# Spreading a recurrence head's steps unevenly over the next projections

## The chip, the cores and the metric

The kernel runs on one core of one Trainium2 chip. The metric is the device time of one launch in microseconds (us). A kernel's figure is the median of several runs. The profile is of one further execution, with a time and a span of its own.

## The reference, cut to what matters

The reference is one inference step of a two-layer decoder trunk for a prompt of 1,024 tokens and 8 sample tokens: first a layer with a gated linear recurrence (HGRN2), then a layer with latent attention, each with a gated feed-forward part behind it. The change touches the first layer's recurrence alone. Its input is projected to four parts (query q, forget gate f, value i, output gate g) of 8 heads of 128. Then per head, in chunks:

```python
b = jnp.cumsum(gc, axis=2)                       # log of the forget gate, summed up
scores = jnp.einsum('bhtk,bhsk,bhtsk->bhts', qc, kc, decay)
o = (jnp.einsum('bhts,bhsv->bhtv', scores, vc)
     + jnp.einsum('bhtk,bhkv->bhtv', qc * jnp.exp(b), s))
s = (jnp.exp(b_last[:, :, 0, :, None]) * s
     + jnp.einsum('bhsk,bhsv->bhkv', kc * jnp.exp(b_last - b), vc))
```

Each head's output is normalised, gated with silu(g), and multiplied by an output matrix.

## The kernel before, in words

The kernel computes in float32. A projection's product is made of three matmuls per 128 rows of the model dimension (lines 181 to 183: both operands are split into a high and a low part). The 1,032 tokens are three spans of 344, so one projection of one span is 24 matmuls. A head has four weights in the order f, q, i, g, and so 12 such projections: f1, f2, f3, q1, q2, q3, i1, i2, i3, g1, g2, g3. In this document "a projection" is one of these 12, and a dash marks those of the next head (f1').

`proj(h)` is a generator with 12 units, one per projection. Each evicts its product on VectorE (L1035). Behind f3 stands a tail that forms b: a chain on ScalarE (L1052 to L1058) and VectorE (L1055 to L1060), and eight scans (L1065). Behind q3 stands a tail of two sigmoids on ScalarE (L1069, L1070) into the tile `sig`, and VectorE products that turn f into k, finish q and close the gate of the head before (L1072 to L1074, L1098). At g1 the values are turned on TensorE (L1087).

`rec(h)` is a generator with 26 steps that does the recurrence of one head, in chunks of 128 tokens, four chunks to a half:

- Seven levels per half (64, 32, 16, 8, 4, 2, 1). For each, `scaled` makes the tile X: a difference of b on VectorE (L1115), two exponentials on ScalarE (L1117), one product on GpSimd (L1118), one on VectorE (L1119). A matmul step of a level (L1129 for 64 and 32, L1145 for the small ones) reads it. `scaled` runs three levels ahead, so step 1 makes four of them, and each of the next steps one.
- `carry` moves the state through a half, in three parts. Part 1: difference (L1164), exponential (L1165), and on GpSimd the product kt (L1166). Part 2: four transposes of kt on TensorE (L1175) and a copy kn on ScalarE (L1177). Part 3: four matmuls with kn (L1182) and the state's update on VectorE (L1192). In half 0 the parts are issued in steps 4, 5 and 6, in half 1 in steps 12, 14 and 15.
- `outs` (L1204, L1206) in steps 12 and 20, and steps 8 and 17 with the level 0.
- `sample` for the 8 sample tokens: the old state is loaded (L1212) into the tile `sv`, scaled and updated (L1215 to L1217) and read by TensorE (L1223), all issued in step 18. Its transposes (L1229) come in step 19. `sv` and `sig` share one buffer (tag "big").
- `norm` in steps 21 to 26, two for each span: square, sum over partitions (L1243), reciprocal root on ScalarE, VectorE products (L1250 to L1252), split (L131 on ScalarE, L132 on GpSimd), stores.

The loop at the end of `hgrn` runs the projections of all heads in order and, behind each, as many recurrence steps as the table 'pace' says, first of the head before, then of the head itself. A head's first steps come behind its own i3, its last behind i3' of the next head: 13 projections. The last head keeps going behind the loop, mixed with products of the output projection.

The instructions are put in an order for each engine by a planner (the `TileContext` of the program is told to schedule with a timeline): instructions issued earlier go first, but one that is not ready in the planner's account can be overtaken. Each engine then runs its list in that order and waits where an operand is late. Buffers that share a tag are handed on when their last reader has finished.

Of the kernel before, what the change touches and what calls it, by code (L numbers as in the profile page):

```python
# [29 lines left out]
H = 8  # L30
# [238 lines left out]
def result(gen):  # L269
# [9 lines left out]
KN = {  # L279
# [3 lines left out]
    'fills': (2, 3, 4, 5, 7, 8, 10, 11, 12, 13),  # L283
    'early': (8, 1),
    'ev': (0, 0, 1),
    'm1': 2,
    'm2': 3,
# [2 lines left out]
    'ho': 1,  # L290
    'groups': ((0, 4), (4, 7), (7, 8)),
    'brate': 2,
    'pace': (8, 26, 13),
    'ahead': 3,
    'pvl': 2,
    'pre': 0,
# [672 lines left out]
def hgrn(k, c, w_in, gnorm, lbl, state, load, st_p, st_s, o_dram, v_dram, out):  # L969
# [13 lines left out]
    with ExitStack() as st:  # L983
# [305 lines left out]
            yield  # L1289
            yield from norm()  # L1290

        (START, STEPS, SPAN), UNITS = KN['pace'], 12
        recs = {}
        for u in range(UNITS * H):
            h, i = divmod(u, UNITS)
            if i == 0:
                units = proj(h)
            next(units)
            if i == UNITS - 1:
                next(units, None)  # L1300
            for j in (h - 1, h):
                n = (u + 1 - UNITS * j - START) * STEPS // SPAN
                if j >= 0 and n > 0:
                    if j not in recs:
                        recs[j] = [rec(j), 0]
                    while recs[j][1] < n:
                        next(recs[j][0], None)
                        recs[j][1] += 1
# [710 lines left out]
def tile_yoco_step(ctx, tc, a, c, o, phases=("hgrn", "ffn0", "mla", "ffn1")):  # L2019
# [21 lines left out]
    for n, ph in enumerate(phases):  # L2041
# [17 lines left out]
        if ph == "hgrn":  # L2059
            od = dram.tile([H, 2, P, T], F32, name="od_a")  # L2060
            vd = dram.tile([H, NB, P], F32, name="vd")
            out = OutProj(k, a["w_out_a"][0], od)
            hgrn(k, c, a["w_in_a"][0], gnorm, lbl, a["state_hgrn"], load, o["state_hgrn_prompt"], o["state_hgrn_sample"], od, vd, out)
            r = out.run(end)
        elif ph == "mla":
            od = dram.tile([H, 2, P, T], F32, name="od_b")
            out = OutProj(k, a["w_out_b"][0], od)

            def first():
                k.accs = ()  # L2070
                k.open_x()
                out.acc = [k.new_acc() for s in range(NS)]
                yield from out.first2(3)

            mla(k, c, a, o, gain(1, 0), cols[:, 64:72], cols[:, 72:74], cols[:, 74:77], r, k.close_x, od, lambda: [out.weight(f) for f in range(3)], first())
            r = out.run(end)
        else:
            r = ffn(k, gated[ph], a["w_ffn_out"][l], g_d, end)
# [69 lines left out]
```

## Time and profile before

| | |
|---|---|
| median of 3 runs | 2902.22 us (2901.31 to 2907.77) |
| the profiled execution, its own time | 2909.61 us |
| its span, first to last instruction | 2907.8 us |
| TensorE (PE) matmul busy | 2735.8 us, 94% |
| VectorE (DVE) / ScalarE (ACT) / GpSimd (POOL) busy | 65% / 44% / 34% |
| mean granted TensorE clock | 0.97 of full speed |

The busy shares are means over the whole span. The recurrence layer is the first fifth of it, and its shares differ from the rest, so it is read by stretches. A wait is given to the instruction that ended last before it. "Granted clock" is the share of TensorE's full clock.

### The profile page before, as it was taken

Reading aid. Unit: us, or ns where it says so; the run is one execution under the profiler, and the core shown is the slowest. Engines: PE = TensorE matmul, PEld = TensorE weight load, DVE = VectorE, ACT = ScalarE, POOL = GpSimd, SP = SyncE. Lnnn points to the kernel's source line nnn. Section 1 sums busy time; section 2 is a strip of 40 time slices with the busy share of each in tenths; the row PEclk is TensorE's granted clock in tenths of the full one; section 3 lists DMA queues with packets and bytes.
Section 4 is the critical chain, followed back from the end, with each engine's and each line's share of the span. In section 5 each row is a group of like instructions: output and inputs, shape, how many; then the busy total and the mean of one; then the engine's idle time right before and its main releaser. Section 6 shows DMA issues by size and latency. Waiting matters only on the chain.

```text
span 2907.8 us, 58217 instructions
## 1 busy us (share of the span) xinstructions
PE 2735.8 (94%) x23252; PEld 2552.8 (88%) x23252; DVE 1880.4 (65%) x3396; ACT 1279.0 (44%) x2888; POOL 983.9 (34%) x894
## 2 busy tenths in 40 slices
PE   7988888889999999999999999878999999998998
PEld 7988888887899999999968899746789999998997
DVE  7888888863585555555568888794358555555555
ACT  7666666654534444400155666523353444440102
POOL 3555555552343323322231111242135333232210
PEclk9999999989999999999999999999999999999999
DMA  5122222153323343544332112586432333436332
GB/s 185 53 68 68 65 68 65 60 185 99 107 91 108 99 114 93 152 160 156 127 99 81 40 45 74 189 335 211 131 106 77 106 105 100 116 118 232 133 124 74
DMA packets 302609, 335.77 MB, mean 115 GB/s; under 512 B 51266, under 2 KB 277104, under 8 KB 290688
## 3 DMA queue, kind: packets, MB, share of 16 engines
q1 hardware_dynamic: 277072, 263.15, 28.9%
q0 software_dynamic: 7456, 43.00, 4.0%
q10 hardware_dynamic: 17808, 25.89, 2.5%
q8 instruction: 183, 3.00, 0.4%
q14 instruction: 90, 0.74, 0.1%
HBM read 241.37 MB, written 90.61 MB: 114 GB/s over the span
## 4 chain that ended last, share of the span: by engine, by line
PE 67%; DVE 13%; ACT 7%; DMA 6%; issue 4%; POOL 2%; SPq 0%; DVEq 0%; POOLq 0%; ACTq 0%
PE ps L181 19%; PE ps L182 18%; PE ps L183 18%; DMA raw<-in_w_ffn_in_dram 3%; PE ps L1700 2%; PE ps L256 1%; DVE w L132 1%; DVE E L1115 1%; PE ps L1627 1%; POOL S L624 1%; DVE X L1119 1%; PE ps L1145 1%; DMA G<-g_d 1%; PE ps L1182 1%; DVE t L659 1%
## 5 line engine op out<-in xcount | busy, mean ns | idle before, releaser
L181 PE MATMUL ps<-xh,w 128*128 128x344 f32 (+1 forms) x2496 | 794.8, 319 | 6.2 <-DVE t L732 2.4
L182 PE MATMUL ps<-xl,w 128*128 128x344 f32 (+1 forms) x2496 | 777.0, 312 | 1.7 <-DVE xl L226 1.6
L183 PE MATMUL ps<-xh,w 128*128 128x344 f32 (+1 forms) x2496 | 772.3, 310 | 0.0
L157 POOL TENSOR_TENSOR w<-raw,w 128x512 fp32r<-128x512 f32 (+1 forms) x216 | 287.6, 1352 | 732.4 <-ACT w L153 715.6
L181 PEld LDWEIGHTS ps<-xh,w 128*128 128x128 f32 x2496 | 478.0, 192 | 29.1 <-issue 12.4
L182 PEld LDWEIGHTS ps<-xl,w 128*128 128x128 f32 x2496 | 477.9, 191 | 14.8 <-issue 6.9
L183 PEld LDWEIGHTS ps<-xh,w 128*128 128x128 f32 x2496 | 477.7, 192 | 6.3 <-issue 6.1
L822 DVE TENSOR_TENSOR acc<-ps,acc 128x344 f32<-128x344 f32 x432 | 222.6, 516 | 197.0 <-PE ps L183 197.0
L181 PE MATMUL ps<-G,w 128*128 128x344 f32 x1008 | 327.5, 325 | 13.6 <-DMA G<-g_d 13.5
L182 PE MATMUL ps<-G,w 128*128 128x344 f32 x1008 | 325.8, 323 | 0.0
L153 ACT CAST w<-raw 128x1024 fp32r<-128x1024 f32 (+4 forms) x134 | 130.2, 974 | 444.2 <-PE ps L183 269.8
L183 PE MATMUL ps<-G,w 128*128 128x344 f32 x1008 | 324.5, 322 | 0.0
L624 POOL TENSOR_TENSOR S<-raw 128x512 f32<-128x512 f32 x72 | 94.4, 1311 | 444.1 <-DMA raw<-in_w_ffn_in_dram 248.3
L132 DVE TENSOR_TENSOR w<-S,w 128x512 fp32r<-128x512 f32 x144 | 157.6, 1104 | 86.9 <-ACT w L131 86.8
L181 PE MATMUL ps<-X,w 128*128 128x258 f32 x720 | 206.4, 287 | 7.3 <-ACT t L721 5.9
L181 PEld LDWEIGHTS ps<-G,w 128*128 128x128 f32 x1008 | 191.6, 190 | 19.6 <-issue 17.8
L182 PE MATMUL ps<-X,w 128*128 128x258 f32 x720 | 204.2, 284 | 0.0
L183 PE MATMUL ps<-X,w 128*128 128x258 f32 x720 | 204.0, 283 | 0.0
L132 DVE TENSOR_TENSOR w<-raw,w 128x512 fp32r<-128x512 f32 x108 | 72.9, 689 | 188.4 <-ACT w L131 182.8
L182 PEld LDWEIGHTS ps<-G,w 128*128 128x128 f32 x1008 | 191.4, 190 | 2.0 <-issue 1.7
L183 PEld LDWEIGHTS ps<-G,w 128*128 128x128 f32 x1008 | 191.6, 190 | 1.1 <-issue 1.1
L181 PEld LDWEIGHTS ps<-X,w 128*128 128x128 f32 x720 | 137.7, 191 | 9.4 <-ACT t L721 6.1
(439 smaller groups left out, 6060.3 us busy)
## 6 DMA issues: line engine op xcount, KB each, us to landing
raw<-in_w_ffn_in_dram SPq DMA_DIRECT2D x88, 512.0 KB
G<-g_d SPq DMA_DIRECT2D x42, 1032.0 KB
g_d<-gs SPq DMA_DIRECT2D x108, 258.0 KB
raw<-in_w_ffn_out_dram SPq DMA_DIRECT2D x44, 512.0 KB
raw<-in_w_in_a_dram SPq DMA_DIRECT2D x32, 512.0 KB
xs<-x_d SPq DMA_DIRECT2D x72, 172.0 KB
x_d<-acc ACTq DMA_DIRECT2D x9, 1376.0 KB
g_d<-gs SPq DMA_DIRECT2D x108, 86.0 KB
```

Of the source, the lines that this page charges most:

```text
L132: (lo_eng or self.nc.vector).tensor_tensor(out=lo, in0=src, in1=hi, op=ALU.subtract)
L153: nc.scalar.copy(wh[:, :n], raw[:, :n])
L157: eng.tensor_tensor(out=wl[:, sl], in0=raw[:, sl], in1=wh[:, sl], op=ALU.subtract)
L181: nc.tensor.matmul(out, lhsT=wh, rhs=ah, start=first and i == 0, stop=False, **skip)
L182: nc.tensor.matmul(out, lhsT=wh, rhs=al, start=False, stop=False, **skip)
L183: nc.tensor.matmul(out, lhsT=wl, rhs=ah, start=False, stop=last and i == n - 1, **skip)
L256: k.nc.tensor.matmul(self.ps[32 * i:32 * i + 32, :W], lhsT=k.one[:, :32], rhs=self.ready[i], start=self.n == 0, stop=self.n == KC - 4, til ...
L624: nc.gpsimd.tensor_tensor(out=src[name], in0=src[a], in1=src[b], op=op)
L659: eng.tensor_tensor(out=part([out]), in0=part(a), in1=part(b), op=op)
L822: nc.vector.tensor_tensor(out=acc[s][:, dc, :], in0=po, in1=acc[s][:, dc, :], op=ALU.add)
L1115: nc.vector.tensor_tensor(out=pairs(E), in0=pairs(bv), in1=ref, op=ALU.subtract)
L1700: return lambda *a, **kw: self.tc.keep_in_program_order(getattr(self.eng, name)(*a, **kw))
```

## The change

The table 'pace' held a start, a number of steps and a span: from the 9th projection of a head on, two recurrence steps behind each projection. Now it holds for each of the 13 projections how many steps have been taken in all. The start and the end stay.

```diff
-    'pace': (8, 26, 13),
+    'pace': (1, 2, 3, 4, 6, 8, 11, 13, 16, 18, 21, 23, 26),
...
-        (START, STEPS, SPAN), UNITS = KN['pace'], 12
+        START, PACE, UNITS = 8, KN['pace'], 12
...
-                n = (u + 1 - UNITS * j - START) * STEPS // SPAN
+                n = u + 1 - UNITS * j - START
+                if n > 0:
+                    n = 2 * n if j == H - 1 or n > len(PACE) else PACE[n - 1]
```

Steps taken behind each projection of a head's run, before and after:

| | i3 | g1 | g2 | g3 | f1' | f2' | f3' | q1' | q2' | q3' | i1' | i2' | i3' |
|---|---|---|---|---|---|---|---|---|---|---|---|---|---|
| before | 1-2 | 3-4 | 5-6 | 7-8 | 9-10 | 11-12 | 13-14 | 15-16 | 17-18 | 19-20 | 21-22 | 23-24 | 25-26 |
| after | 1 | 2 | 3 | 4 | 5-6 | 7-8 | 9-11 | 12-13 | 14-16 | 17-18 | 19-21 | 22-23 | 24-26 |

The last head (j = H - 1) keeps two steps per projection. No instruction is added, removed or altered; only the order of issue changes.

## Rows read from the trace of the kernel before

**Rows 1.** Busy time by engine, with granted clock (PEclk), in two stretches of the span.

```profile
75.00:580.00 505.00, 458.34 (x5557) 429.41 (x5556) 414.59 (x642) 313.36 (x659) 268.61 (x217) 0.94 0.21 64
...
645.00:2908.00 2263.00, 2162.40 (x16581) 2016.67 (x16580) 1363.32 (x2571) 872.37 (x2044) 652.16 (x621) 0.98 0.38 123
```

**Rows 2.** TensorE's waits, 74 to 600 us: total, times, longest.

```profile
PE ps L1175 <- POOL kt L1166: 42.4, 8, 5.9
PE ps L1182 <- ACT kn L1177: 10.2, 8, 1.4
```

**Rows 3.** Busy time in six successive heads, from a third i projection's end to the next.

```profile
209.50:283.56 74.06, 66.73 (x810) 62.43 (x809) 60.60 (x94) 45.60 (x97) 39.70 (x33) 0.93 0.22 66
...
sum 444.30, PE 399.99 PEld 374.17 DVE 364.06 ACT 275.20 POOL 239.23; mean PE 66.67 PEld 62.36 DVE 60.68 ACT 45.87 POOL 39.87
```

**Rows 4.** Timeline of TensorE around one wait (start, duration, instruction, idle before).

```profile
221.04 0.44 PE L1145 MATMUL ps<-X 128*32 128x32 f32 x26
227.36 1.11 PE L1175 MATMUL ps<-ident,kt 128*128 128x128 f32 x4 [5.88 <-POOL kt L1166]
230.12 2.08 PE L1182 MATMUL ps<-vn,kn 128*128 128x128 f32 x8 [1.39 <-ACT kn L1177]
232.71 0.66 PE L181 MATMUL ps<-xh,w 128*128 128x344 f32 x1
237.89 0.46 PE L1145 MATMUL ps<-X 128*32 128x32 f32 x32
...
243.52 0.43 PE L181 MATMUL ps<-xh,w 128*128 128x344 f32 x1
247.50 0.46 PE L1145 MATMUL ps<-X 128*32 128x32 f32 x32
...
258.66 1.05 PE L1182 MATMUL ps<-vn,kn 128*128 128x128 f32 x8
```

**Rows 5.** Timeline of VectorE and GpSimd behind that wait.

```profile
222.42 0.68 DVE L1164 TENSOR_TENSOR E<-b 128x512 f32<-128x512 f32 x1
224.09 0.41 DVE L1119 TENSOR_TENSOR X<-lin,E 128x256 f32<-128x256 f32 x1
226.12 1.46 DVE L1119 TENSOR_TENSOR X<-lin,E 128x256 f32<-128x256 f32 x1 [0.82 <-ACT E L1117]
...
224.82 1.26 POOL L132 TENSOR_TENSOR ol<-oy,oh 128x344 fp32r<-128x344 f32 x1 [1.02 <-issue]
226.05 1.25 POOL L1166 TENSOR_TENSOR kt<-lin,E 128x512 f32<-128x512 f32 x1
```

**Rows 6.** Busy time and clock behind head 0's waits, and behind that of rows 4.

```profile
82.00:90.50 8.50, 8.39 (x69) 7.89 (x72) 8.50 (x13) 2.13 (x7) 5.07 (x5) 0.61 0.01 2
230.12:232.20 2.08, 2.08 (x13) 1.86 (x17) 2.08 (x3) 0.56 (x2) 2.07 (x3) 0.50 0.03 8
```

**Rows 7.** TensorE's waits in head 0, 60 to 137 us.

```profile
PE ps L1182 <- ACT kn L1177: 1.2, 1, 1.2
PE ps L1175 <- POOL kt L1166: 1.1, 1, 1.1
```

**Rows 8.** VectorE by line in one head, 209.5 to 283.56 us.

```profile
L1119 DVE TENSOR_TENSOR X<-lin,E 128x256 f32<-128x256 f32 x14 | 13.6, 990 | 1.0 <-ACT E L1117 0.8 <-PE ps L1129 0.2
L1115 DVE TENSOR_TENSOR E<-b 128x512 f32<-128x512 f32 x14 | 12.1, 880 | 0.2
...
L1035 DVE TENSOR_TENSOR lin<-ps,r 128x344 f32<-128x344 f32 x9 | 4.6, 507 | 5.3 <-PE ps L183 5.3
```

**Rows 9.** The state's load, the end of the gate, and the product that reads the state.

```profile
199.87 1.77 DVE L1098 SCALAR_TENSOR_TENSOR lin<-lin,gains,sig 128x1032 f32<-128x1032 f32 x1
201.78 0.37 SPq L1212 DMA_DIRECT2D sv<-in_state_hgrn_dram  x1
...
L1223 PE MATMUL ps<-sv,qpad x16: 272/273/295, 264.6 to 265.0; 128*32 128x128 f32 x16
L1215 POOL TENSOR_TENSOR sv<-sv,fs x1: 1962/1962/1962, 205.8 to 205.8; 128x1024 f32<-128x1024 f32 x1
```

## The prediction

> **What bounds the kernel now.** I read by stretches first. In the recurrence layer TensorE is busy 458 of 505 us at a granted clock of 0.94, behind it 96% at 0.98 [rows 1]. So the layer's heads, about 74 us each, are where TensorE stands still. TensorE's own waits come next: between 74 and 600 us nearly all of them have two names, the transposes of kt (42.4 us in 8) and the matmuls on kn (10.2 us in 8) [rows 2]. The timeline of one head gives their place. The transposes of half 0, issued in step 5 behind g2, wait 5.88 us. The kn matmuls behind them wait 1.39 us. Then the clock is down: the kn matmuls take 2.08 us where later ones take 1.05, and the projection behind (first matmul to what follows) 237.89 - 232.71 = 5.18 us where another takes 247.50 - 243.52 = 3.98 [rows 4]. The granted clock there is 0.50, the 1.2 GHz level, after TensorE stood idle for most of 9 us [rows 4, 6]. So one head loses 5.9 + 1.4 = 7.3 us in waits and 1.0 + 1.2 + about 0.2 for the small matmuls = 2.4 us in clock, together 9.7. That fits the head's length: 444.30 / 6 = 74.05 us, of which TensorE is busy 66.67 [rows 3], and 66.67 - 2.4 = 64.3 is its work at full clock.
>
> Why kt is late is seen on VectorE and GpSimd. VectorE comes to the carry's difference (L1164) only at 222.42, with TensorE idle since 221.48 [rows 4, 5]. GpSimd makes kt at 226.05, behind the split (L132, 224.82) of the norm of the head before [rows 5]. VectorE is busy 60.60 us of this head's 74.06, and 5.3 us of its rest lie before evictions, where it waits for TensorE [rows 3, 8]. The wait is thus a crowd: in two projections (i3, g1) the table before issues the first four steps, that is seven of the fourteen level tiles, beside the norm of the head before. One level costs VectorE (13.6 + 12.1) / 14 = 1.84 us [rows 8], so seven cost 12.9, and TensorE's projection lasts 3.98.
>
> **What the change does, part by part.** Nothing is added or removed; the sum is made of waits and clock.
>
> *Step 5, half 0.* It moves from behind g2 to behind f1', step 4 (which makes kt) from behind g1 to behind g3. TensorE has the same steps before it, and two projections more: it comes to the transposes not at 221.48 but 2 x 3.98 later, at 229.4. kt was ready at 226.05 + 1.25 = 227.3 [rows 4, 5]. VectorE has two more evictions before it (0.51 each [rows 8]): 228.3. So the 5.9 us go, with a margin of 1.1 us that the planner's order may eat. Bounds for what is left: 0 and 5.9; I take 0.3, near the computed end.
>
> *Step 6.* It stays behind the same projection as step 5, so the copy kn still stands between them with little to cover it. Bounds 0 and 1.4; I take 1.0, nearest to the row.
>
> *Half 1.* Steps 14 and 15 were behind different projections and are now behind one (q2'). So a wait like that of step 6 is added: 0 to 1.4, I take 0.6, since step 16's matmuls are issued there too and can be put between. The tiles of the second half are now made beside the tail behind f3', a long chain on ScalarE and VectorE, where before they lay ahead of it. Steps 9 to 11 add three levels, 5.5 us, there. The cover is that half 1's kt is still issued a whole projection ahead of its transposes; if it is gone, this is the wait of half 0 in a new place (the second rival's kind).
>
> *The clock.* In head 0 two short waits of 1.1 and 1.2 us [rows 7] are followed by a clock of 0.61 over 8.5 us [rows 6], so short waits can cost it too. Bounds 0 and 2.4, I take 1.2.
>
> *Queues.* No DMA is added; step 18's loads on SP are the ones that could move (second rival). GpSimd's products go with their levels, 39.70 us busy of 74.06 [rows 3], so room is left.
>
> What stays is 0.3 + 1.0 + 0.6 + 1.2 = 3.1 us a head, the gain 9.7 - 3.1 = 6.6. Six heads' waits (heads 1 to 6) are of the full kind: 39.6. Head 0 has 2.3 us of wait and, as in the others, about 2.4 of clock; I take half, 2.4. Head 7 keeps its old table, but shares i3 with three last steps of head 6 instead of two: it loses 0 to 1, I take 0.5. Sum 41.5 us. Nothing behind the layer hides it: TensorE is 96% busy there [rows 1], so what it saves is saved at the end. The profiled execution's 2909.61 becomes 2868; that execution lies 7.4 us over the median of the runs, 2902.22, which becomes 2861.
>
> **The rivals.**
>
> *VectorE becomes the bound.* Its 60.68 us of work a head [rows 3] don't shrink. Of its idle 13.4 us, 5.3 are waits for TensorE, which a faster TensorE takes away; the other 8.1 are waits on ScalarE and gaps. If those stay, a head can't fall below 60.7 + 8.1 = 68.8 us: a gain of 5.2 a head, 31 in six, 2871. If the new crowd behind f3' and q3' adds 3 us of waits to that, 72 us a head and some 2889. For it speaks that 60.7 us of work must fit beside TensorE's 64.3; against it, that the levels issued beside f3' can fill the waits of its chain on ScalarE. A page of the Trainium skill, GPSIMD Engine Reference, Specifications, says that GpSimd and VectorE share their way into SBUF, so that two-input VectorE instructions are slowed. By it the change, which takes away none of GpSimd's work, leaves VectorE's time as it is, and the end would be this rival's 2871. The trace agrees: the same product took 0.41 us with GpSimd idle and 1.46 us beside kt [rows 5].
>
> *Slower: the state's load goes behind the sigmoids.* `sv` and `sig` have one buffer. Before, step 18 was issued behind q2', ahead of the sigmoids of q3'; the load goes out at 201.78, as soon as the gate (L1098) has read `sig` at 201.64, 63 us ahead of the matmuls at 264.6 [rows 9]. Now step 18 is issued behind q3' and its tail. If the buffer is then handed out in order of issue, the load waits for the gate that follows q3'. That is 4.2 us or more behind q3': between its end and i3's end at 209.50 [rows 3] lie three projections, so it ended at 209.50 - 11.9 = 197.6 at the latest, and the load went out at 201.78. GpSimd's first product (L1215) began 4.0 us behind the load and took 1.96, and a second of the same size follows [rows 9]. So L1223 could start 4.2 + 4.0 + 1.96 + 1.96 = 12.1 us behind q3', and held in its place it costs that and 2.4 of clock, 14.5, for 9.7 saved: 4.8 a head lost, 34 in seven, 2936. It turns the sign from a wait of 7.3 us on. Against it: the load is taken far ahead of its issue, and the planner can put projections in front of a product that it knows to be late. Then it costs little.
>
> *No change.* The planner already takes work out of issue order (26 of the 32 records of step 5's small matmuls stand ahead of the transposes that it issues first [rows 4]). If it again leaves the first levels crowded, or the same wait comes back in half 1 (6 + 1.4 + 2.4), the time stays within some us of 2902.
>
> **How the numbers follow.** A measurement of this kernel tells 0.2%, about 6 us, from no change. Forecast, 2845 to 2875: 0.50. VectorE as the bound with waits left, 2875 to 2896: 0.27. No change, 2896 to 2908: 0.08. Slower by the load or a larger wait in half 1, 2908 to 2955: 0.15. So faster 0.77, same 0.08, slower 0.15. The range is 2845 to 2902: it leaves out the slower case and half of the unchanged one, 0.19.
>
> **What would show it.** In the changed profile: L1175 should wait under 1 us a head in place of 5.9, L1182 at most 1.4 in either half; the stretch behind should hold a clock of 1.00; a head from i3 to i3 should last 66 to 69 us with TensorE's work unchanged; VectorE's waits before evictions should shrink from 5.3 us. I am wrong if a new wait of over 3 us a head stands at L1175 behind q2', at L1223 or at L1204 behind i1', if the load L1212 is issued behind the gate of the next head, or if the slow clock stays although the waits are short.

## The result, and the profile after

The changed kernel takes 3052.95 us (median of 5 runs, 3049.72 to 3055.16) against 2902.22 (2901.31 to 2912.1): a ratio of 1.051, 95% interval 1.0496 to 1.0523. It is 151 us slower, where 41 us faster was forecast.

| | before | after |
|---|---|---|
| the profiled execution, its own time | 2909.61 us | 3053.28 us |
| its span | 2907.8 us | 3051.5 us |
| TensorE (PE) matmul busy | 2735.8 us, 94% | 2748.7 us, 90% |
| VectorE / ScalarE / GpSimd busy | 65% / 44% / 34% | 60% / 44% / 32% |
| mean granted TensorE clock | 0.97 | 0.951 |

The first view is busy time by stretches: one head of the changed kernel (start, end and length; then busy time of PE, PEld, DVE, ACT and POOL; then clock, DMA share, GB/s), the gap in it, and the projection behind the gap.

```profile
140.85:236.74 95.89, 69.23 (x811) 64.96 (x807) 56.00 (x93) 54.33 (x103) 38.44 (x32) 0.86 0.16 51
219.56:235.73 16.17, 0.00 (x1) 0.00 (x1) 5.74 (x8) 7.18 (x10) 7.95 (x5) 0.60 0.32 97
236.74:242.30 5.56, 5.56 (x31) 5.54 (x28) 0.04 (x1) 0.47 (x2) 0.00 (x0) 0.71 0.33 94
```

A head lasts 95.9 us at a clock of 0.86, where before it lasted 74.05 at 0.93 [rows 3]. For 16.2 us TensorE runs nothing, and the projection behind the gap takes 5.56 us. From one head's third i eviction to the next the trace has 95.6 us in the mean ((634.74 - 252.37) / 4); (95.6 - 74.05) x 7 heads = 151, about the whole loss. Work was added on ScalarE alone: 54.33 us busy in 103 instructions against 45.60 in 97 [rows 3].

TensorE's waits, 60 to 800 us (total, times, longest), answer to [rows 2, 7]:

```profile
PE ps L1223 <- POOL sv L1217: 113.9, 7, 16.6
PE ps L1182 <- ACT kn L1177: 72.5, 15, 7.1
PE ps L1175 <- POOL kt L1166: 3.5, 1, 3.5
```

The wait that the change was to remove is removed: 42.4 us for kt are now 3.5, and those are the last head's, which keeps its old table. But the kn matmuls wait 72.5 us instead of 10.2, and the state's matmuls, which did not wait, wait 113.9. The timeline of several engines shows how that big wait comes about (start, duration, engine, instruction, idle time before it and what ended that).

```profile
224.67 1.29 DVE L1098 SCALAR_TENSOR_TENSOR lin<-lin,gains,sig 128x1032 f32<-128x1032 f32 x1
...
226.09 0.37 SPq L1212 DMA_DIRECT2D sv<-in_state_hgrn_dram  x1
...
230.22 1.89 POOL L1215 TENSOR_TENSOR sv<-sv,fs 128x1024 f32<-128x1024 f32 x1 [2.89 <-DMA sv<-in_state_hgrn_dram]
...
231.46 1.73 DVE L1216 TENSOR_TENSOR sv<-sv,lin 128x1024 f32<-128x1024 f32 x1 [4.91 <-issue]
...
233.34 2.34 POOL L1217 TENSOR_TENSOR sv<-sv 128x1024 f32<-128x1024 f32 x1 [1.23 <-DVE sv L1216]
...
235.73 1.08 PE L1223 MATMUL ps<-sv,qpad 128*32 128x128 f32 x16 [16.17 <-POOL sv L1217]
```

The load of the state (L1212) leaves 0.13 us behind the end of the gate (224.67 + 1.29 = 225.96), as in [rows 9]. But the gate is now the one that follows q3', and the matmuls that need the load come next on TensorE, not 63 us later. From TensorE's last matmul ahead of the gap (219.56, of a step issued behind q3') to the load are 6.5 us, from there to GpSimd's first product 4.1, from there to the end of its second 5.5. No projection was put in front.

The timeline of ScalarE ahead of that, and behind it TensorE's row for half 1's kn:

```profile
193.77 0.63 ACT L1057 ACTIVATE tw<-tw 128x516 f32<-128x516 f32 x1
194.42 1.28 ACT L1069 ACT_TABLE_LOAD   x1
195.71 1.07 ACT L1069 ACTIVATE sig<-lin 128x1032 f32<-128x1032 f32 x1
...
197.47 1.28 ACT L1058 ACT_TABLE_LOAD   x1
198.77 0.63 ACT L1058 ACTIVATE tw<-tw 128x516 f32<-128x516 f32 x1
199.42 1.28 ACT L1165 ACT_TABLE_LOAD   x1
...
203.21 1.28 ACT L1054 ACT_TABLE_LOAD   x1
...
205.95 1.28 ACT L1167 ACT_TABLE_LOAD   x1
...
210.76 0.57 ACT L1177 COPY kn<-ps 128x512 f32<-128x512 f32 x1
211.35 1.28 ACT L1058 ACT_TABLE_LOAD   x1
...
211.38 2.08 PE L1182 MATMUL ps<-vn,kn 128*128 128x128 f32 x8 [7.07 <-ACT kn L1177]
```

The forecast had no term for this. The first sigmoid (L1069, into `sig`) now runs in the middle of f3''s chain of logarithms (L1054, L1058) and of exponentials (L1057, L1165 and L1167 among them). The kernel names one common activation table for those two in the line behind the sigmoids (L1071); ahead of it each change of kind costs a table load of 1.28 us. Four such loads lie between the sigmoid and the copy kn, and L1182 waits 7.07 us. The groups of table loads by line, of the kernel before and then of the changed one (times, busy time, mean ns of one), 75 to 700 us:

```profile
L1069 ACT ACT_TABLE_LOAD x7 | 9.0, 1283 | 0.1
L1071 ACT ACT_TABLE_LOAD x7 | 9.0, 1283 | 0.1
```

```profile
L1058 ACT ACT_TABLE_LOAD x14 | 18.0, 1283 | 0.2
L1069 ACT ACT_TABLE_LOAD x7 | 9.0, 1283 | 0.1
L1165 ACT ACT_TABLE_LOAD x7 | 9.0, 1283 | 0.1
L1054 ACT ACT_TABLE_LOAD x7 | 9.0, 1283 | 0.1
...
L1070 ACT ACT_TABLE_LOAD x7 | 9.0, 1283 | 0.1
```

Nine a head instead of two. Before, `sv` held the shared buffer until its matmuls (264.6, [rows 9]), so the sigmoids could not be early; in the runs below that issue step 18 or its load ahead of them again, the loads are back at two a head.

### The profile page after: what moved, and what is told of

Same layout as the page of the kernel before. It is cut to its first block, busy times and chain, and to the rows that moved or that the text cites. A ratio compares the mean times of both kernels' runs of the same rounds, so it can differ in the third digit from the quotient of the medians.

```text
span 3051.5 us, 58227 instructions
## 1 busy us (share of the span) xinstructions
PE 2748.7 (90%) x23252; PEld 2566.4 (84%) x23252; DVE 1845.6 (60%) x3396; ACT 1340.3 (44%) x2937; POOL 972.6 (32%) x894
## 4 chain that ended last, share of the span: by engine, by line
PE 60%; DVE 14%; ACT 12%; DMA 7%; issue 5%; POOL 3%; SPq 0%; DVEq 0%; POOLq 0%; ACTq 0%
PE ps L181 17%; PE ps L182 16%; PE ps L183 16%; DMA raw<-in_w_ffn_in_dram 3%; PE ps L1702 2%; DVE t L659 2%; PE ps L256 1%; DVE E L1115 1%; DVE X L1119 1%; DVE w L132 1%; PE ps L1629 1%; POOL S L624 1%; ACT E L1117 1%; DMA G<-g_d 1%; PE ps L1182 1%
## 5 line engine op out<-in xcount | busy, mean ns | idle before, releaser
L157 POOL TENSOR_TENSOR w<-raw,w 128x512 fp32r<-128x512 f32 (+1 forms) x216 | 295.2, 1387 | 714.5 <-ACT w L153 693.0
L181 PEld LDWEIGHTS ps<-xh,w 128*128 128x128 f32 x2496 | 484.3, 194 | 28.4 <-issue 13.2
L182 PEld LDWEIGHTS ps<-xl,w 128*128 128x128 f32 x2496 | 484.9, 194 | 14.2 <-issue 7.2
L183 PEld LDWEIGHTS ps<-xh,w 128*128 128x128 f32 x2496 | 483.2, 194 | 6.3 <-issue 6.1
L132 DVE TENSOR_TENSOR w<-S,w 128x512 fp32r<-128x512 f32 x144 | 157.6, 1104 | 82.2 <-ACT w L131 82.1
L132 DVE TENSOR_TENSOR w<-raw,w 128x512 fp32r<-128x512 f32 x108 | 73.0, 690 | 189.5 <-ACT w L131 184.1
L1118 POOL TENSOR_TENSOR X<-lin,E 128x256 f32<-128x256 f32 x112 | 105.0, 946 | 146.4 <-PE ps L1145 56.0
```

The costliest lines, as they stand in the source:

```text
L132: (lo_eng or self.nc.vector).tensor_tensor(out=lo, in0=src, in1=hi, op=ALU.subtract)
L157: eng.tensor_tensor(out=wl[:, sl], in0=raw[:, sl], in1=wh[:, sl], op=ALU.subtract)
L181: nc.tensor.matmul(out, lhsT=wh, rhs=ah, start=first and i == 0, stop=False, **skip)
L182: nc.tensor.matmul(out, lhsT=wh, rhs=al, start=False, stop=False, **skip)
L183: nc.tensor.matmul(out, lhsT=wl, rhs=ah, start=False, stop=last and i == n - 1, **skip)
L1118: nc.gpsimd.tensor_tensor(out=Xl[:, :, 0, :], in0=kl[:, :, 0, :], in1=El[:, :, 0, :], op=ALU.mult)
```

## The experiments

Some of the experiments ran beside a kernel before of 2902 to 2903 us, others (e4, e5, e7, e8, e13) beside one of 2915 to 2918. So runs of the two groups are compared by their ratios to the kernel before measured beside each.

### Step 18 back behind q2', and step 18 alone behind q3'

The first kernel takes step 18 out of the change, the second keeps nothing else of it.

```diff
-    'pace': (1, 2, 3, 4, 6, 8, 11, 13, 16, 18, 21, 23, 26),
+    'pace': (1, 2, 3, 4, 6, 8, 11, 13, 18, 18, 21, 23, 26),   # e1_step18_before
+    'pace': (2, 4, 6, 8, 10, 12, 14, 16, 17, 20, 22, 24, 26),  # e2_only18_late
```

> The changed table with one entry altered: behind q2' 18 steps are taken in all instead of 16, so that step 18 (the state's load into the buffer that sv and sig share) is issued ahead of q3' and its sigmoids again; all else as in the change. Theory A (the handing on of the shared buffer is the whole loss): L1223's wait of 16.2 us a head goes, the six to seven extra table loads a head on ScalarE go with it, L1182's 7.1 us behind q2' fall under 2, and the gain of the spread start appears: 2850 to 2885 us. Rival B (the crowd behind f3' and q1' to q2' is a loss of its own): L1223's wait goes, but L1182 still waits 5 to 7 us behind q2' and the clock stays down there: 2900 to 2960 us.

Measured: 2935.63 us, ratio 1.0114 (1.0092 to 1.0136). The waits of the first, 75 to 760 us:

```profile
PE ps L1182 <- ACT kn L1177: 81.1, 15, 8.1
PE ps L1175 <- POOL kt L1166: 4.0, 1, 4.0
```

L1223's wait is gone and the table loads are two a head again. That takes back 117 of the 151 us, but the rest of the table does not gain: it loses 33 us, in the range of rival B, since kn is waited for in both halves (8.0 us a head in half 0, 4.4 in half 1; rival B had put the larger wait in half 1). The timeline of ScalarE, VectorE and TensorE in half 0 of one head:

```profile
239.17 0.76 ACT L1117 ACTIVATE E<-E 128x256 f32<-128x256 f32 x2 [2.44 <-DVE E L1115]
241.94 0.42 ACT L1117 ACTIVATE E<-E 128x256 f32<-128x256 f32 x1 [2.00 <-DVE E L1115]
...
244.44 0.72 ACT L1117 ACTIVATE E<-E 128x256 f32<-128x256 f32 x2 [0.85 <-DVE E L1115]
246.12 0.72 ACT L1117 ACTIVATE E<-E 128x256 f32<-128x256 f32 x2 [0.95 <-DVE E L1115]
246.87 0.59 ACT L1177 COPY kn<-ps 128x512 f32<-128x512 f32 x1
...
237.72 4.19 DVE L1115 TENSOR_TENSOR E<-b 128x512 f32<-128x512 f32 x2
...
243.67 2.36 DVE L1115 TENSOR_TENSOR E<-b 128x512 f32<-128x512 f32 x2
...
238.50 0.60 PE L1175 MATMUL ps<-ident,kt 128*128 128x128 f32 x4
...
247.51 1.86 PE L1182 MATMUL ps<-vn,kn 128*128 128x128 f32 x7 [8.02 <-ACT kn L1177]
```

The transposes are done at 239.1. The copy that takes them over needs 0.59 us, but it stands on ScalarE behind the exponentials of four levels (L1117), each of which waits for a difference of VectorE (L1115), and a cast of a weight between them (1.03 us). It comes 7.8 us late. TensorE no longer waits for VectorE through kt; it waits for VectorE through ScalarE's queue.

> The table of before, two steps behind each projection, with one entry altered: behind q2' 17 steps in all instead of 18, so that only step 18 moves behind q3'. Theory A: this alone brings the loss: L1223 waits 14 to 17 us a head, the first sigmoid is taken early into the free buffer and ScalarE loads tables six to seven times more a head, the old wait of L1175 behind g2 stays in part: 3000 to 3060 us. Rival B: only L1223's wait comes, no wait of over 2 us at L1182 in half 1: 2990 to 3020 us. If the late step 18 were not the cause: 2895 to 2915 us.

Measured: 3054.86 us, ratio 1.0521 (1.0496 to 1.0547). The waits, 75 to 760 us:

```profile
PE ps L1223 <- POOL sv L1217: 156.0, 7, 22.4
PE ps L1175 <- POOL kt L1166: 20.7, 8, 4.0
PE ps L1182 <- ACT kn L1177: 13.1, 8, 2.5
```

One step moved by one projection brings a loss as large as that of the whole change, though with a longer wait (22.3 us a head) and with part of the old one for kt. The trace has eight table loads a head here.

### The first sigmoid kept in its place

The changed kernel, with the first sigmoid kept in program order on ScalarE.

```diff
-   nc.scalar.activation(out=sig[:, 0, :], in_=f, func=AF.Sigmoid, scale=-1.0)
+   tc.keep_in_program_order(nc.scalar.activation(out=sig[:, 0, :], in_=f, func=AF.Sigmoid, scale=-1.0))
```

> The changed kernel, with the first sigmoid (L1069) pinned behind everything issued before it on ScalarE, so that it can't be taken early; the order of the shared buffer stays that of the change. Theory A: table loads go back to two a head, L1182's wait behind q2' falls from 7.1 us to under 2, L1223's wait of about 16 us stays: 2985 to 3025 us. Rival B (the wait at L1182 comes from the crowd of levels and not from the loads): L1182 keeps 5 to 7 us: 3035 to 3060 us.

Measured: 3030.2 us, ratio 1.044 (1.0411 to 1.047). Two table loads a head; the waits, 75 to 760 us:

```profile
PE ps L1223 <- POOL sv L1217: 107.0, 7, 15.4
PE ps L1182 <- ACT kn L1177: 54.7, 15, 4.4
```

The early sigmoid with its seven extra loads a head costs 23 of the 151 us (3052.95 - 3030.2), above all through half 1's kn, whose wait falls from 7.1 to 4.4 us. That is less than was expected; the order in which the buffer is handed on is the larger part.

### The buffer taken earlier, the matmuls left where the change puts them

The changed table, but `sv` is taken from the pool and its loads are issued in step 15; products and matmuls stay in step 18.

```diff
+            def fetch():
                 big_ = gp.tile([P, 3, T], F32, name="sv", tag="big")
...
+                state_["sv"] = S0, vB
+
             def sample():
+                S0, vB = state_["sv"]
...
+                if (hf, hh) == (1, 2):
+                    fetch()
```

> The changed table as it is, step 18 behind q3' as in the change, but the shared buffer is taken for sv and the two loads into it are issued in step 15 (behind q2', ahead of the sigmoids of q3'); the products on it and L1223 stay in step 18. Theory A (the order in which the one buffer is handed on is the cause, not the place of step 18's matmuls): L1223 waits under 2 us a head, ScalarE loads tables twice a head, and the time is within 1% of the run with step 18 moved whole (ratio 1.0114): 1.004 to 1.020. Rival: the products behind q3' or L1223's place cost it, L1223 keeps 5 us or more a head and the ratio stays over 1.025.

Measured: 2975.21 us, ratio 1.0205 (1.0179 to 1.0232), a hair above the expected bound of 1.020. The loads go out far ahead again, behind the gate of the head before, as [rows 9] (the queue's own row), and of the waits, 75 to 760 us, L1223's is gone (lines behind 1213 are shifted by 4: L1233 is L1229, L1229 is L1225):

```profile
217.96 0.37 SPq L1212 DMA_DIRECT2D sv<-in_state_hgrn_dram  x1
```

```profile
PE ps L1182 <- ACT kn L1177: 75.6, 15, 7.4
PE ps L1233 <- ACT so L1229: 15.2, 7, 2.2
```

The table loads are two a head. So the issue order of the two users of one buffer is the cause of the wait, and not that step 18 lies behind q3' as such; that place costs the remaining per cent over the first experiment (2.2 us a head of it are the wait for `so`, the copy of what L1223 made).

### What makes kn late

First, step 6 a projection behind step 5, and the second half as before:

```diff
-    'pace': (1, 2, 3, 4, 6, 8, 11, 13, 18, 18, 21, 23, 26),   # the first experiment's
+    'pace': (1, 2, 3, 4, 5, 8, 11, 13, 18, 18, 21, 23, 26),   # e4_step6_apart
+    'pace': (1, 2, 3, 4, 6, 8, 11, 14, 18, 20, 22, 24, 26),   # e5_old_tail
```

> The table of the run with step 18 ahead of q3' (2935.6 us), and step 6 moved from behind f1' to behind f2' with steps 7 and 8, so that a whole projection lies between the transposes of kt and the matmuls on kn. Theory C (the wait only went from kt to its copy kn, because steps 5 and 6 share a projection and the copy stands behind exponentials on ScalarE): L1182's 8.0 us in half 0 fall to between 1 and 4.5, a head gets 3 to 6 us shorter, 2895 to 2918 us. Rival D (VectorE is late at this place whatever the order, and what is won at kn is lost at the next level's matmuls): other waits of the same sum appear at L1145 or L1129, 2925 to 2945 us.

> The spread start of the change (steps 1 to 11 as there), and from q1' on the table of before: steps 12 to 14 behind q1', 15 to 18 behind q2', then two each. So the carry of half 1 has its transposes and its kn matmuls behind different projections and the norm comes where it came before. Theory C: the 4.4 us of L1182 in half 1 go, the 8.0 of half 0 stay or shrink by 1 to 3 because the norm is off VectorE earlier: 2895 to 2915 us. Rival D: half 0 keeps its 8 and half 1 gets another wait: 2925 to 2945 us.

Measured: 2922.82 us, ratio 1.0029 (1.0019 to 1.0039), and 2922.96 us, ratio 1.0026 (1.0012 to 1.0041). By the ratios both fall where theory C put them (2895 to 2918 and 2895 to 2915 beside 2902), and neither gains on the kernel before. In e4_step6_apart half 0's wait for kn falls from 8.0 us to 5.2, above the expected 4.5, though a whole projection now lies between the transposes and the matmuls, and half 1 keeps 4.2. In e5_old_tail half 1's falls from 4.4 to 1.3, and half 0 keeps 6.7. That leaves some 61 and 50 us of wait for kn between 75 and 585.

Then the first experiment's table, with the exponentials of later levels kept behind the kn copy on ScalarE:

```diff
-   nc.scalar.activation(out=El[:, :, i, :], in_=El[:, :, i, :], func=AF.Exp, scale=sign)
+   with tc.issue_after(state_["kn"]) if state_["kn"] is not None else ExitStack():
+       nc.scalar.activation(out=El[:, :, i, :], in_=El[:, :, i, :], func=AF.Exp, scale=sign)
...
-   nc.scalar.copy(kn, pt)
+   state_["kn"] = nc.scalar.copy(kn, pt).ins
```

> The table of the run with step 18 ahead of q3' (2935.6 us), and on ScalarE the exponentials of the levels issued behind the copy kn are kept behind it. Theory C: the copy no longer stands behind exponentials that wait for VectorE, L1182's 8.0 us in half 0 fall under 2.5, at half 1 (4.4) less changes because there the copy also stands behind the chain of f3'; 2880 to 2910 us. Rival D: the exponentials are now late in their place, and the level's matmuls L1145 wait for what L1182 no longer does: 2920 to 2945 us.

Measured: 2919.19 us, ratio 1.0013 (1.0003 to 1.0023). The timeline of TensorE and ScalarE in half 0 (L1176, L1178 and L1183 are L1175, L1177 and L1182):

```profile
231.53 0.60 PE L1176 MATMUL ps<-ident,kt 128*128 128x128 f32 x4
...
235.48 1.16 PE L1183 MATMUL ps<-vn,kn 128*128 128x128 f32 x8 [2.96 <-ACT kn L1178]
...
232.85 1.03 ACT L153 CAST w<-raw 128x1024 fp32r<-128x1024 f32 x1
234.41 0.40 ACTq L1219 DMA_DIRECT2D out_dram<-sv  x1
234.84 0.58 ACT L1178 COPY kn<-ps 128x512 f32<-128x512 f32 x1 [0.96 <-POOL sv L1218]
```

With the later exponentials out of the copy's way, 8.02 us become 2.96, and the matmuls take 1.16 us for eight instead of 1.86 for seven: the granted clock there is 1.00 instead of 0.50. The wait left is above the 2.5 us that were expected: between the transposes and the copy still stand two exponentials issued before it, a cast of a weight and a store of `sv` that waits for GpSimd. Half 1 still waits 4.4 to 5.5 us.

### Tables that keep some of the spread

A start two projections earlier, so that all has more room; a table that only holds step 5 back by one projection; that with the pin of the experiment above; and a slow start with everything from step 8 on in its old place.

```diff
-        START, PACE, UNITS = 8, KN['pace'], 12
+        START, PACE, UNITS = 6, KN['pace'], 12                        # e7_early_start
...
-                    n = 2 * n if j == H - 1 or n > len(PACE) else PACE[n - 1]
+                    n = 2 * n - 4 if j == H - 1 or n > len(PACE) else PACE[n - 1]   # e7_early_start
...
-    'pace': (1, 2, 3, 4, 6, 8, 11, 13, 16, 18, 21, 23, 26),
+    'pace': (1, 2, 3, 4, 5, 6, 8, 10, 12, 14, 18, 20, 22, 24, 26),   # e7_early_start
+    'pace': (2, 4, 4, 5, 8, 12, 14, 16, 18, 20, 22, 24, 26),         # e9_hold_step5, e10_hold_and_pin
+    'pace': (1, 2, 3, 4, 8, 12, 14, 16, 18, 20, 22, 24, 26),         # e11_slow_then_old
```

> Not an undoing but the idea of the change taken further: the recurrence starts two projections earlier (behind i1 in place of i3), one step each up to g3, two each from f1' on, step 18 behind q2', the tail as before; the last head keeps two per projection from i3 on. Steps 4, 5 and 6 are each a projection apart. Theory C: no wait of over 1.5 us at L1175 or L1182, the clock stays up, 2850 to 2880 us. Rival D (VectorE and its share with GpSimd bound the head): 2880 to 2905 us, with waits at the level's matmuls (L1129, L1145).

> The table of before with steps 5 and 6 held back alone: 2, 4, 4, 5, 8, 12 steps in all behind i3, g1, g2, g3, f1', f2', then as before. kt is issued where it was (behind g1), its transposes come one projection later (g3) and the kn matmuls one more (f1'); half 1, the state's load and the norm keep their places. Theory C (waits at single places, which a later consumer cures): L1175's 5.9 us fall to 1 to 3 and L1182's 1.4 go, with the slow clock behind them; a head 5 to 9 us shorter, 2 to 1% off the time of before: ratio 0.980 to 0.990. Rival D (VectorE has no room in this stretch, and the wait only changes its name): ratio 0.995 to 1.005, with new waits at L1145, L1129 or L1204.

> As the run with steps 5 and 6 held back, and the exponentials of levels issued behind a copy kn kept behind it on ScalarE. Theory C: the copy has a whole projection already, so the pin adds little: ratio 0.978 to 0.992, within 0.4% of the run without it. Rival D: the pinned exponentials make the next levels late, 1.000 to 1.010.

> The spread start of the change up to g3 (one step each), then four steps each behind f1' and f2', and from there the table of before: half 1's carry, the state's load and the norm are where they were before. Theory C: steps 5 and 6 share f1' with 7 and 8, so the wait at kn in half 0 stays (3 to 8 us), half 1 has none: ratio 0.995 to 1.005. Rival D: the same wait, and a further one at outs (L1204) or in half 1 because four steps' levels are crowded: 1.005 to 1.015.

| | us | ratio (interval) | TensorE's largest waits, longest of one |
|---|---|---|---|
| e7_early_start | 2930.77 | 1.0057 (1.0040 to 1.0074) | the norm's sum L1243, 4.3 us |
| e9_hold_step5 | 2886.19 | 0.9944 (0.9930 to 0.9957) | kt 2.5 us in heads 1 to 6, kn 0.8 to 3.6 |
| e10_hold_and_pin | 2899.27 | 0.9984 (0.9975 to 0.9993) | the copy A for L1204, 4.5 us; kt 2.5 |
| e11_slow_then_old | 2887.50 | 0.9947 (0.9934 to 0.9961) | kn of half 0, 6.6 to 6.9 us; kt none but the last head's |

Two beat both kernels, by half a per cent, with intervals clear of 1. e9_hold_step5 lies between what its two theories expected (0.980 to 0.990 and 0.995 to 1.005), and e7_early_start is slower than either of its own. The busy times of one head of e9_hold_step5 are:

```profile
204.55:274.48 69.93, 64.79 (x812) 61.06 (x807) 62.38 (x94) 45.20 (x96) 40.56 (x33) 0.98 0.24 70
```

Here 5.88 us of wait for kt have become 2.5, kn's 1.39 have become 2.2, and the clock of the head goes from 0.93 to 0.98. VectorE is busy 62.38 of 69.93 us. What e7_early_start moves comes back as a wait in the norm, and what e10_hold_and_pin takes from kn it gives to A.

## Why the prediction was wrong

**The step that failed most is the weighing of the second rival.** Its mechanism was named and is what happened: the load stands behind the gate that follows q3'. Three things in it were wrong. It was given 0.15, because the planner "can put projections in front of a product that it knows to be late"; the trace shows TensorE with no work for 16.2 us and the projection behind L1223. The step took an ability of the planner for what it would do here, and no row of before showed a projection moved across such a wait. Its price was low: 12.1 us were said, 6.5 + 4.1 + 5.5 = 16.1 measured. Load to first product is right (4.0 against 4.1). The stretch from q3' to the gate was a bound "4.2 or more", taken at its low end: it holds the sigmoids with their table loads and two products of VectorE of 1.2 to 1.3 us each. The trace of before had its length, in the eviction of q3' on VectorE:

```profile
195.50 0.51 DVE L1035 TENSOR_TENSOR lin<-ps,r 128x344 f32<-128x344 f32 x1
```

The load at 201.78 [rows 9] is 6.3 us behind that; in the changed trace the same stretch is 226.09 - 219.20 = 6.9. And the products do not follow each other: L1216 on VectorE (1.73) lies between them, and L1217 took 2.34. Last, from the price it took 9.7 us of gain, which was not there. So even this rival's range, 2908 to 2955, ends far below the 3053 measured.

**The gain failed by itself, without step 18.** The sum of the forecast left 3.1 us a head. Kt's 5.9 us went as said (step 5, right), but "Step 6 ... I take 1.0" and "Half 1 ... 0.6" were bounded by 1.4, the row of before, and e1_step18_before measured 8.0 and 4.4. That bound was the step that failed here: a wait for a copy is not bounded by one copy with a free ScalarE. The copy waits for its engine's queue, and the queue waited for VectorE. VectorE's lateness, which the forecast saw (seven levels beside a norm), did not go when the transposes came later; they only stopped being the first to feel it. e8_kn_first shows the queue as the cause in half 0: the copy put first, 8.0 becomes 3.0. The clock was taken at 1.2 us a head; with waits of 8 us it falls as low as before (0.50 over the kn matmuls of that timeline, as in [rows 6]).

The loss of 21.6 us a head can be laid out by head lengths, taken from one third i eviction to the next in each trace: 74.05 before; 78.7 in e1_step18_before, +4.6, kn behind ScalarE's queue; 82.0 in e13_load_early, +3.3, the later place of step 18's products and matmuls; 95.6 after, +13.6, the buffer handed on late, with the early sigmoid's table loads in it (23 / 7 = 3.3). By the ratios (their differences times 2902 us, over seven heads) the three parts are 4.7, 3.8 and 12.6. The last is less than L1223's 16.2 us though the table loads are in it. What fits is that VectorE catches up in that pause, since half 0's kn waits 3.4 us in the changed kernel and 7.2 in e13_load_early; no run tested that.

**What held.** TensorE's work in a head at full clock was worked out as 64.3 us; e9_hold_step5 shows 64.79 at 0.98. The first rival, VectorE as the bound, said that a head can't fall below 60.7 + 8.1 = 68.8 us; heads 1 to 5 of e9_hold_step5 take 70.0 to 70.9 us and head 6 takes 68.8, by their third i evictions, and in the view above VectorE is idle for 7.5. None of heads 1 to 6 in any table tried here goes clearly below that floor, and it rather than the forecast's 66 to 69 fits them. That VectorE sets it is argued from its busy share; no run took work from VectorE. The prediction's own signs of error (a wait of over 3 us at L1223; the load behind the next gate) are the ones that stand in the trace.

**Open.** Of the 3.3 us that step 18's place costs beside the load, 2.2 are the wait for `so`; that the sigmoids now wait for L1223 to read the buffer, and the rest of the head with them, is argued and not shown. Why the norm's square is late in e7_early_start was not followed. The clock's own share in the 13.6 us was not measured apart.

## What to carry to other kernels

Before a step is moved in an order of issue, list each buffer that it shares with another user and ask which of the two is now issued first: moving one step past the sigmoids turned a load that was 63 us early into a wait of 16.2 us, and taking the buffer in an earlier step undid it. A wait that ends at a late engine isn't removed by issuing its first victim later: look for the next instruction that stands in order behind that engine's results, here a copy of 0.6 us on ScalarE that came 7.8 us late. When an activation can be taken early into a chain of others, look at what tables they use.

## What the runs showed of the hardware

- An activation table load took 1283 ns each time. The Trainium skill, ScalarE: Activation LUTs, What ACT_TABLE_LOAD costs, gives 1283 ns and a drain of 1.38 us beside it, 2.66 us for a switch. The trace agrees with the first figure and shows no drain here: L1069's load begins at 194.42, the exponential before it ends at 193.77 + 0.63 = 194.40, and the sigmoid starts at 195.71, so the measured price is 1.3 us from the one to the other. The Trainium skill's rule on that page to batch activations by table set (Table sets: the hidden batching unit) fits what e3_sigmoid_pinned gained, 23 us with seven loads a head fewer.
- In e1_step18_before two differences (L1115) took 4.19 us beside GpSimd's L132 and L1217, two took 2.36 us a few us later beside its L157, and one with GpSimd idle took 0.69. The price of a VectorE instruction with two inputs depended on what it met, as in [rows 5].
